# A hybrid decoder block on one core: in the MLP's first pass the product S1·T1 third and S2·T2 fourth, and a GpSimd power planned at 1.2 instead of 0.35

## The chip, the core and the metric

The kernel runs on one core of a Trainium2 chip. The metric is the device time of one execution in microseconds (us). Before the change it is 1147.73 us, the median of three runs (1147.73 to 1148.61). In this text TensorE is PE in the profile, VectorE is DVE, ScalarE is ACT, GpSimd is POOL, and SP is the engine whose queue issues the DMAs.

## What is computed

One decoder block over 1024 tokens of width 1024 with float32 data. `rms_norm` is x / sqrt(mean(x²) + eps) times a gain, and `sh`, `sc` and `gt` are shifts, scales and gates that a small product makes of the conditioning vector.

```python
h = rms_norm(x, g_attn_pre[l]) * (1 + sc_a) + sh_a
proj = h @ w_in[l]
...
mixed = jnp.concatenate([rms_norm(oa, g_mix_a[l]), rms_norm(ob, g_mix_b[l])], axis=-1)
y = mixed @ w_out[l]
x = x + gt_a * rms_norm(y, g_attn_post[l])

h = rms_norm(x, g_mlp_pre[l]) * (1 + sc_m) + sh_m
...
```

The last lines of the layer are the MLP: h times `w_up` (1024 x 4096), squared ReLU, times `w_down` (4096 x 1024), then a norm, a gate and a residual sum. oa and ob are the outputs of two kinds of attention.

## The kernel before

**Products.** Each float32 factor is split into a high part (a cast to the format fp32r, which TensorE multiplies) and a low part (the factor less its high part). A product is then three matmuls: high by high, high by low and low by high. High parts are casts on ScalarE (L1666 for a whole tile, L1664 for a piece of its columns); low parts are subtractions on VectorE (L1673, L1670). The function `split` makes both.

**Scheduling.** The program is written out by a list scheduler, the class `Sched`. Each piece of work is given to it by `op` (for ScalarE, VectorE, GpSimd), `pe_op` or `dense` (TensorE) or `load` (DMA), with the work that it depends on, the buffers that it takes and gives back, a priority and a duration that the author entered. The scheduler keeps a clock for each engine, and when an engine is free it appends the work that can start by these durations, by priority. Its choices fix the order of the instructions on each engine; on the chip every engine runs its own list in that order, and semaphores hold an instruction until what it needs is there. The planned durations have no other effect on what is executed.

**Output projection.** `out_block(tb)` is called for each of eight blocks of 128 tokens. For a block it loads the attention's output (`o_sb`), casts it on ScalarE (L1436), takes its low part on VectorE (L1439), squares it on ScalarE (L1441), sums on VectorE (L1445, L1446) and on TensorE (the matmuls `pm_o`, L1452), and after a small VectorE instruction (L1460) raises two columns to the power -1/2 on GpSimd (`rab`, L1462, planned at 0.5). TensorE makes y in tiles of 12 matmuls (L1478 to L1480); ScalarE (L1493) and VectorE (L1499) read them, scaled by `rab`. Then comes twice the helper `norm`: a sum of squares on ScalarE (L1506), a small VectorE instruction (L1515) and a power of one column on GpSimd (L1517, planned at 0.35). Between the two stand L1521 (scale and gate) and L1524 (add the residual x), after the second L1532 (`xn`, the scaled row). TensorE transposes xn (`px`, L1541, 8 matmuls), and VectorE or ScalarE writes the eight pieces of h, each with a scale and a shift (L1560, L1557). The blocks overlap, and the last ones overlap with the start of the MLP.

**MLP.** w_up and w_down are worked off in eight passes ("halves", h = 0 to 7), alternately a part of w_up and a part of w_down. In a pass both factors are 2 x 2 blocks, and instead of eight block products there are seven, P1 to P7, with sums of blocks as their factors (Winograd's variant of Strassen's scheme): `OPERANDS` names the pair of each, S for sums of the left factor's blocks, T for the right one's. S1 = A21 + A22, S2 = S1 - A11, S3 = A11 - A21, T1 = B12 - B11, T2 = B22 - T1. A product is 48 matmuls (L1902, L1903, L1904), in four PSUM banks (m = 0 to 3) by four blocks of the inner dimension. `ORDER` is the order of the products in a pass. In the first pass the left factor is h itself, so S1, S2 and S3 are made while the last h pieces are still coming. `first_sums` makes S1 (L1792) and S2 (L1797) in two pieces of columns, 384 and 128 wide per row of 512 (`PIECES`), for each of two halves j of the inner dimension, so that a part of each can be cast before the last token block is there; S3 is L1815. All other sums of blocks are whole tiles (`add_up`, L1835). The products' banks are read by `read_up` (ScalarE L1936, L1941, L1942 and VectorE L1939). The high and low parts of the left factor in the first pass are stored to DRAM by `store_parts` and loaded again in later passes. The tiles of w are loaded into a ring of buffers, and a slot is free when the sum or the split that reads it last is done.

In the first pass P2 runs bank by bank. `ml.seq` is the list of all products; `product` calls `sums` and `prep` for a product, `prep` calls `split`, and the priority of both follows from the product's place in `ml.seq`.

Of the kernel before, what the change touches and what calls it, by code (L numbers as in the profile page):

```python
# [20 lines left out]
D = 1024  # L21
# [327 lines left out]
def hybrid_block(ctx: ExitStack, tc: tile.TileContext, x, positions, w_ada, b_ada, g_attn_post, w_in, w_out,  # L349
# [1066 lines left out]
    def out_block(tb):  # L1416
# [92 lines left out]
        def norm(col, dep):  # L1509
            bx = []  # L1510

            def f1():
                t = small.tile([P, 8], F32, name="rs_t", tag="rs_t")
                bx.append(t)
                V.tensor_scalar(t[:, :1], b["st"][:, col:col + 1], 1.0 / D, EPS, ALU.mult, ALU.add)  # L1515
            e = op("DVE", 0.08, f1, [dep], prio=0)
            return op("POOL", 0.35, lambda: G.tensor_tensor(b["st"][:, col + 1:col + 2], bx[0][:, :1], nhalf[:, :1],  # L1517
                                                            ALU.pow), [e], prio=0)
        e = op("ACT", t_sb(D) + AP_COST, f_sq(0, True), ey, prio=1)
        e = norm(0, e)  # L1520
# [66 lines left out]

    NW = 4
    ORDER = ("P1", "P2", "P6", "P5", "P7", "P3", "P4")
    LAST = ("P1", "P2", "P6", "P5", "P3", "P7", "P4")  # L1590
    CHAIN = ("P1", "P6", "P7", "P4")
    OPERANDS = dict(P1=("11", "11"), P2=("12", "21"), P6=("S2", "T2"), P5=("S1", "T1"), P7=("S3", "T3"),
# [2 lines left out]
    BANKS = ([(pj, "pj", r_pj)] * 2 + [(psp, "s", r_s)] * 2,  # L1595
             [(po, "o", r_o), (px, "x", r_x), (pt, "t", r_t), (pt, "t", r_t)])
    ml = Tok()
    ml.seq = [(h, p) for h in range(2 * NW) for p in (ORDER if h < 2 * NW - 1 else LAST)]
    ml.fed = ml.begun = ml.done = 0
    ml.y, ml.e_y, ml.st = {}, {}, {}  # L1600
    halves = {}
    e_sd = {}
# [50 lines left out]
    def split(prio, rec, side, src, deps, free, pieces=None):  # L1653

        out = rec.hl[side] = [None, None]
        evs = [None, None]
        for i, c in enumerate(pieces or (slice(0, 512),)):
            for j in range(2):
                def hi(i=i, j=j, c=c):
                    if not i:  # L1660
                        i_, out[j] = new_pair()
                        rec.join[j].n.append(i_)
                    if pieces:
                        A.copy(halves_of(out[j][0])[:, :, c], pair(src[j])[:, :, c])  # L1664
                    else:
                        A.copy(out[j][0], flat(src[j]))  # L1666

                def lo(j=j, c=c):
                    if pieces:
                        V.tensor_tensor(halves_of(out[j][1])[:, :, c], pair(src[j])[:, :, c],  # L1670
                                        halves_of(out[j][0])[:, :, c].bitcast(F32), ALU.subtract)
                    else:
                        V.tensor_tensor(out[j][1], flat(src[j]), out[j][0].bitcast(F32), ALU.subtract)  # L1673

                def after(j=j):
                    for n in free:
                        n[j].hit()
                n = 2 * (c.stop - c.start)
                d = [deps(j)[i]] if pieces else deps(j)
                e1 = op("ACT", t_as(n), hi, d + (evs[j] or []), takes=[] if i else [(r_hl, 1)], prio=prio)  # L1680
                evs[j] = [e1, op("DVE", t_dv(n), lo, [e1], prio=prio,
                                 after=after if c.stop == 512 else None)]
        return evs
# [22 lines left out]
    def sums(h, p):  # L1706

        t = half(h)
        fr = t.free
        up_ = h % 2 == 0  # L1710
        own_a = h == 0 or not up_
        if p == "P1":
            fr.update({"T1": joins(r_raw, 2), "T3": joins(r_raw, 1), "B22": joins(r_raw, 3), "T4": joins(r_raw, 1),
                       "T2": joins(r_raw, 2)})
            if h == 0:
                t.a = {q: h2[q] for q in h2}
                t.e_a = dict(e_h2)
# [12 lines left out]
        ea, eb = events(h)  # L1730
        sum_ = partial(add_up, 10 + ml.seq.index((h, p)))
        if p == "P6":
            sum_(t.b, t.e_b, eb, r_raw, None, "T1", "12", "11", ALU.subtract, [], t.sp["B", "11"], "11")
            sum_(t.b, t.e_b, eb, r_raw, ring_r, "T2", "22", "T1", ALU.subtract, [fr["B22"], fr["T1"]], None, None)
            if h == 0:
                first_sums(t)
            elif own_a:
                sum_(t.a, t.e_a, ea, t.ring, t.new, "S1", "21", "22", ALU.add, [fr["A22"]], None, None)
                sum_(t.a, t.e_a, ea, t.ring, None, "S3", "11", "21", ALU.subtract, [], [[e] for e in t.e_a["S1"]], "21")
                sum_(t.a, t.e_a, ea, t.ring, None, "S2", "S1", "11", ALU.subtract, [fr["S1"]],  # L1740
                     [x + [t.e_a["S3"][j]] for j, x in enumerate(t.sp["A", "11"])], "11")
        if p == "P7":
            sum_(t.b, t.e_b, eb, r_raw, None, "T3", "22", "12", ALU.subtract, [fr["B22"]], [[e] for e in t.e_b["T1"]],
                 "12")
        if p == "P3" and own_a:
            sum_(t.a, t.e_a, ea, t.ring, None, "S4", "12", "S2", ALU.subtract, [fr["S2"]], t.sp["A", "12"], "12")
        if p == "P4":
            sum_(t.b, t.e_b, eb, r_raw, None, "T4", "21", "T2", ALU.subtract, [fr["T2"]], t.sp["B", "21"], "21")

    def prep(h, p, rec):  # L1750
# [11 lines left out]
        t.sp["B", b] = eB  # L1762
        if own_a:
            fa = [fr["A22"]] if a == "22" else [fr[a]] if a[0] == "S" else []
            eA = split(pr, rec, "A", t.a[a], (lambda j: t.e_a["S2"][j::2]) if (h, a) == (0, "S2") else ea(a), fa,
                       PIECES if (h, a) == (0, "S2") else None)
            t.sp["A", a] = eA
        else:
            eA = load_parts(rec, p)
# [9 lines left out]

    def first_sums(t):  # L1780

        pr = 10 + ml.seq.index((0, "P6"))
        for q in ("S1", "S2"):
            t.a[q] = [None, None]
        t.e_a.update(S1=[], S2=[], S3=[])
        last = {}
        for i, c in enumerate(PIECES):
            for j in range(2):
                def f_s1(i=i, j=j, c=c):
                    if not i:  # L1790
                        t.a["S1"][j] = ring_r("sum_S1")
                    V.tensor_tensor(pair(t.a["S1"][j])[:, :, c], t.a["21"][j][:, :, c], t.a["22"][j][:, :, c], ALU.add)  # L1792

                def f_s2(i=i, j=j, c=c):
                    if not i:
                        t.a["S2"][j] = ring_l("sum_S2", F32)
                    V.tensor_tensor(pair(t.a["S2"][j])[:, :, c], pair(t.a["S1"][j])[:, :, c], t.a["11"][j][:, :, c],  # L1797
                                    ALU.subtract)

                def after(i=i, j=j):  # L1800
                    if i:
                        t.free["S1"][j].hit()
                e1 = op("DVE", t_dv(2 * (c.stop - c.start)), f_s1, [t.e_a[q][2 + i] for q in ("21", "22")] +
                        [x for x in [last.get((1, j))] if x], takes=[] if i else [(r_h2, 1)], prio=pr,
                        after=t.free["A22"][j].hit if i else None)
                e2 = op("DVE", t_dv(2 * (c.stop - c.start)), f_s2, [e1, t.e_a["11"][3]] +
                        [x for x in [last.get((2, j))] if x], takes=[] if i else [(r_u, 1)], prio=pr, after=after)
                last[1, j], last[2, j] = e1, e2
                t.e_a["S2"].append(e2)
                if i:  # L1810
                    t.e_a["S1"].append(e1)
        t.a["S3"] = t.a["21"]
        for j in range(2):
            def f_s3(j=j):
                V.tensor_tensor(flat(t.a["21"][j]), flat(t.a["11"][j]), flat(t.a["21"][j]), ALU.subtract)  # L1815

            def after(j=j):
                sc_give(r_h2)
            t.e_a["S3"].append(op("DVE", t_dv(D), f_s3, [t.e_a["S1"][j]] + t.sp["A", "11"][j], prio=pr + 0.6,
                                  after=after))  # L1820

    def sc_give(r):
        r.give(sc.end)
# [44 lines left out]
    def product(h, p):  # L1868
# [7 lines left out]
        rec.join = [Join(None, [], 3 if h == 0 else 1) for _ in range(2)]  # L1876
        if not q:
            sums(h, p)
        prep(h, p, rec)
        ch = 0 if p in CHAIN else 1  # L1880
        banks = BANKS[ch if up_ else 1 - ch]
        starts, ends = p in ("P1", "P2", "P5"), p in ("P2", "P3", "P4")
# [197 lines left out]
```

## Time and profile before

| | |
|---|---|
| median of 3 runs | 1147.73 us |
| profiled execution, its own time | 1148.87 us |
| span of the profiled execution | 1147.1 us |
| mean granted TensorE clock | 0.992 |
| out of the seven products of the eight passes: matmuls on L1902, L1903 and L1904 | 896 each |
| power L1517: count, mean | 16, 838 ns |
| power L1462: count, mean | 8, 700 ns |

The times in the views are microseconds from the start of the span, unless they are marked ns. A row of a timeline has the start, the duration, the engine, the line, the operation, the tile written and those read, the shapes and a count of instructions that followed one another; a bracket has the idle time before and what ended it. A row of a group has the count, the busy time, the mean of one in ns and the idle time before with its releasers. Matmuls are pipelined, so consecutive matmuls overlap in the records and their distance is the difference of the starts. A row of the windows has the stretch, its length, the busy time of PE, PEld (the loading of weights), DVE, ACT and POOL with their counts, the granted clock of TensorE, the DMA share and GB/s.

### The profile page before, as it was taken

What the parts mean: (1) busy time and instruction counts of PE and PEld (TensorE: products, weight loads), DVE (VectorE), ACT (ScalarE), POOL (GpSimd) and SP (SyncE); (2) the same over time, 40 slices, a digit from 0 to 9 for tenths busy, and PEclk for the clock granted to TensorE, in tenths of its full rate; (3) what the DMA queues carried; (4) which work ended last, traced back from release to release, by engine and by line L of the source; (5) the groups of instructions that cost most, each with busy time, mean ns of one, the idle gap of its engine ahead of it and who ended that gap; (6) DMA issues with size and microseconds to landing.
All of it is one profiled execution on the core that took longest, in us unless ns stands there. A gap on an engine that the chain in (4) does not pass through costs nothing.

```text
span 1147.1 us, 15609 instructions
## 1 busy us (share of the span) xinstructions
PE 1115.2 (97%) x5417; PEld 924.1 (81%) x5417; DVE 818.7 (71%) x1380; ACT 635.9 (55%) x1101; POOL 265.7 (23%) x349
## 2 busy tenths in 40 slices
PE   8999999999999899998999999999999999999996
PEld 7788878888888687887788888888888888888885
DVE  7878666666667765668979664599644896537998
ACT  8868865464556756675675424563234733246542
POOL 2458867565743521111000000000000000000002
PEclk9999999999999899998999999999999999999999
DMA  9556454343423305552981168812469112584103
GB/s 347 192 204 164 163 158 164 136 155 127 146 71 132 124 26 186 203 207 104 352 306 39 41 224 285 303 37 74 147 230 332 70 56 76 201 307 168 37 19 147
DMA packets 90910, 185.29 MB, mean 162 GB/s; under 512 B 8400, under 2 KB 31056, under 8 KB 90832
## 3 DMA queue, kind: packets, MB, share of 16 engines
q1 hardware_dynamic: 90832, 184.30, 46.3%
q8 instruction: 43, 0.70, 0.2%
q14 instruction: 35, 0.29, 0.1%
HBM read 137.08 MB, written 28.31 MB: 144 GB/s over the span
## 4 chain that ended last, share of the span: by engine, by line
PE 76%; DVE 8%; issue 4%; ACT 4%; POOL 4%; DMA 3%; SPq 1%; DVEq 0%; POOLq 0%; ACTq 0%
PE mlp_ps L1903 16%; PE mlp_ps L1904 16%; PE mlp_ps L1902 16%; PE pj L866 3%; PE pj L869 3%; PE pj L867 3%; PE s_ps L1127 3%; PE o_ps L1262 2%; PE pt_ps L1232 1%; PE y_ps L1478 1%; PE y_ps L1480 1%; PE y_ps L1479 1%; PE pt_ps L1235 1%; DVE hw L1673 1%; PE o_ps L1267 1%
## 5 line engine op out<-in xcount | busy, mean ns | idle before, releaser
L1902 PE MATMUL mlp_ps<-hw 128*128 128x512 f32 x896 | 350.7, 391 | 0.4 <-ACT hw L1664 0.4
L1903 PE MATMUL mlp_ps<-hw 128*128 128x512 f32 x896 | 349.5, 390 | 1.1 <-DVE hw L1670 1.1
L1904 PE MATMUL mlp_ps<-hw 128*128 128x512 f32 x896 | 349.4, 390 | 0.0
L1903 PEld LDWEIGHTS mlp_ps<-hw 128*128 128x128 f32 x896 | 168.7, 188 | 36.9 <-DVE hw L1670 1.4
L1902 PEld LDWEIGHTS mlp_ps<-hw 128*128 128x128 f32 x896 | 168.8, 188 | 36.4 <-ACT hw L1664 0.8
L1904 PEld LDWEIGHTS mlp_ps<-hw 128*128 128x128 f32 x896 | 168.6, 188 | 35.0
L1673 DVE TENSOR_TENSOR hw<-w,hw 128x1024 fp32r<-128x1024 f32 x96 | 114.7, 1221 | 95.1 <-ACT hw L1666 93.0
L1666 ACT CAST hw<-w 128x1024 fp32r<-128x1024 f32 x96 | 97.5, 1047 | 129.8 <-PE mlp_ps L1904 93.1
L2002 POOL TENSOR_TENSOR st<-st,nhalf 128x1 f32<-128x1 f32 x8 | 7.8, 977 | 604.1 <-DVE st L2000 604.1
L866 PE MATMUL pj<-hw,w_hl 128*128 128x512 f32 x240 | 102.5, 427 | 0.0
L869 PE MATMUL pj<-hw,w_hl 128*128 128x512 f32 x240 | 94.6, 394 | 0.0
L867 PE MATMUL pj<-hw,w_hl 128*128 128x512 f32 x240 | 94.5, 394 | 0.0
L1250 DVE TENSOR_TENSOR ph<-pt_ps,ph 128x512 fp32r<-128x512 f32 (+1 forms) x110 | 69.5, 648 | 34.6 <-ACT ph L1246 34.3
L1666 ACT CAST hw<-u 128x1024 fp32r<-128x1024 f32 x48 | 48.7, 1051 | 64.6 <-PE mlp_ps L1904 64.6
L1246 ACT CAST ph<-pt_ps 128x512 fp32r<-128x512 f32 (+1 forms) x110 | 58.9, 555 | 32.9 <-PE pt_ps L1235 27.5
L1153 ACT ACTIVATE p_sb<-p_sb,mn 128x128 f32<-128x128 f32 (+3 forms) x64 | 49.8, 778 | 38.3 <-DVE mn L1146 36.8
L1673 DVE TENSOR_TENSOR hw<-u,hw 128x1024 fp32r<-128x1024 f32 x48 | 57.1, 1220 | 18.2 <-ACT hw L1666 18.2
L1960 DVE TENSOR_TENSOR yacc<-yacc,mlp_ps 128x512 f32<-128x512 f32 x96 | 62.2, 683 | 3.3 <-PE mlp_ps L1904 3.3
L1158 POOL TENSOR_SCALAR p_sb<-p_sb,den 128x128 f32<-128x128 f32 (+3 forms) x64 | 48.4, 762 | 53.1 <-DVE den L1156 51.9
L1015 POOL TENSOR_TENSOR ada_acc<-ada_acc,wa_st 128x512 f32<-128x512 f32 x42 | 55.3, 1318 | 3.5
L869 PEld LDWEIGHTS pj<-hw,w_hl 128*128 128x128 f32 x240 | 45.1, 188 | 10.5
L1478 PE MATMUL y_ps<-hw,oh 128*128 128x512 f32 x128 | 51.7, 404 | 0.0
(206 smaller groups left out, 2010.4 us busy)
## 6 DMA issues: line engine op xcount, KB each, us to landing
hw<-s_dram SPq DMA_DIRECT2D x84, 512.0 KB, 4.4
wa_st<-in_w_ada SPq DMA_DIRECT2D x32, 512.0 KB, 4.4
w<-in_w_up SPq DMA_DIRECT2D x32, 512.0 KB, 4.8
w<-in_w_down SPq DMA_DIRECT2D x32, 512.0 KB, 7.5
s_dram<-hw SPq DMA_DIRECT2D x28, 512.0 KB, 4.3
qt<-hl SPq DMA_DIRECT2D x40, 256.0 KB, 2.8
w_st<-in_w_in SPq DMA_DIRECT2D x36, 256.0 KB, 3.1
x_sb<-in_x SPq DMA_DIRECT2D x16, 512.0 KB, 6.1
```

What stands on the lines that cost most here:

```text
L866: T.matmul(ps, w[:, 0, n], h[0], start=(k == 0), stop=False)
L867: T.matmul(ps, w[:, 1, n], h[0], start=False, stop=False)
L869: T.matmul(ps, w[:, 0, n], h[1], start=False, stop=(k == KC - 1))
L1246: A.copy(b["ph"][:, 0, :w], b["pt"][:, :w])
L1250: V.tensor_tensor(b["ph"][:, 1, :w], b["pt"][:, :w], b["ph"][:, 0, :w].bitcast(F32), ALU.subtract)
L1478: T.matmul(ps[:], b["oh"][:, k], wh[:, c0:c0 + 512], start=(k == 4 * m), stop=False)
L1666: A.copy(out[j][0], flat(src[j]))
L1673: V.tensor_tensor(out[j][1], flat(src[j]), out[j][0].bitcast(F32), ALU.subtract)
L1902: T.matmul(ps[m][:], sh, mh, start=starts and k == 0, stop=False, **kw)
L1903: T.matmul(ps[m][:], sh, ml_, start=False, stop=False, **kw)
L1904: T.matmul(ps[m][:], sl, mh, start=False, stop=k == 3, **kw)
L1960: e = op("DVE", t_dv(512), lambda: V.tensor_tensor(y(), y(), ps[m][:], ALU.add), [e, ml.e_y[tb, n]], gives=gives, prio=1)
```

## The change

The first pass has an order of its own, `FIRST_UP`, in which P5 (S1·T1) is third and P6 (S2·T2) fourth; the other passes keep theirs. T1's sum goes with P5 in the first pass. `first_sums` is cut in two: S1, in its two pieces of columns, is made ahead of P5; `second_sums` makes S2, now as two whole tiles, and S3 behind it. `prep` splits S1 in pieces in place of S2. In `split`, for priorities below 17 (products in the first pass), the first casts of a product depend, for the scheduler, on the first casts of the product before it having been placed (`ml.turn`, `rec.turn`); this makes no semaphore. Both powers of `norm` (L1517) are planned at 1.2 instead of 0.35.

```diff
-            return op("POOL", 0.35, lambda: G.tensor_tensor(b["st"][:, col + 1:col + 2], bx[0][:, :1], nhalf[:, :1],
+            return op("POOL", 1.2, lambda: G.tensor_tensor(b["st"][:, col + 1:col + 2], bx[0][:, :1], nhalf[:, :1],
...
     ORDER = ("P1", "P2", "P6", "P5", "P7", "P3", "P4")
+    FIRST_UP = ("P1", "P2", "P5", "P6", "P7", "P3", "P4")
...
-    ml.seq = [(h, p) for h in range(2 * NW) for p in (ORDER if h < 2 * NW - 1 else LAST)]
+    ml.seq = [(h, p) for h in range(2 * NW) for p in (FIRST_UP if not h else ORDER if h < 2 * NW - 1 else LAST)]
+    ml.turn = []
...
+        turn = ml.turn if prio < 17 else []
...
-                e1 = op("ACT", t_as(n), hi, d + (evs[j] or []), takes=[] if i else [(r_hl, 1)], prio=prio)
+                mine = Ev()
+                if not i:
+                    rec.turn.append(mine)
+                e1 = op("ACT", t_as(n), hi, d + (evs[j] or turn), takes=[] if i else [(r_hl, 1)], prio=prio,
+                        after=partial(setattr, mine, "t", 0.0))
...
+        if p == ("P6" if h else "P5"):
+            sum_(t.b, t.e_b, eb, r_raw, None, "T1", "12", "11", ALU.subtract, [], t.sp["B", "11"], "11")
+            if not h:
+                first_sums(t)
         if p == "P6":
-            sum_(t.b, t.e_b, eb, r_raw, None, "T1", "12", "11", ALU.subtract, [], t.sp["B", "11"], "11")
             sum_(t.b, t.e_b, eb, r_raw, ring_r, "T2", "22", "T1", ALU.subtract, [fr["B22"], fr["T1"]], None, None)
             if h == 0:
-                first_sums(t)
+                second_sums(t)
...
-            eA = split(pr, rec, "A", t.a[a], (lambda j: t.e_a["S2"][j::2]) if (h, a) == (0, "S2") else ea(a), fa,
-                       PIECES if (h, a) == (0, "S2") else None)
+            eA = split(pr, rec, "A", t.a[a], (lambda j: t.e_s1[j::2]) if (h, a) == (0, "S1") else ea(a), fa,
+                       PIECES if (h, a) == (0, "S1") else None)
...
-                def f_s2(i=i, j=j, c=c):
-                    if not i:
-                        t.a["S2"][j] = ring_l("sum_S2", F32)
-                    V.tensor_tensor(pair(t.a["S2"][j])[:, :, c], pair(t.a["S1"][j])[:, :, c], t.a["11"][j][:, :, c],
-                                    ALU.subtract)
...
+    def second_sums(t):
+
+        pr = 10 + ml.seq.index((0, "P6"))
+        t.a["S2"] = [None, None]
+        t.e_a.update(S2=[], S3=[])
         t.a["S3"] = t.a["21"]
+        for j in range(2):
+            def f_s2(j=j):
+                t.a["S2"][j] = ring_l("sum_S2", F32)
+                V.tensor_tensor(t.a["S2"][j][:], flat(t.a["S1"][j]), flat(t.a["11"][j]), ALU.subtract)
+            t.e_a["S2"].append(op("DVE", t_dv(D), f_s2, [t.e_a["S1"][j], t.e_a["11"][3]], takes=[(r_u, 1)], prio=pr,
+                                  after=t.free["S1"][j].hit))
...
+        rec.turn = []
         prep(h, p, rec)
+        ml.turn = rec.turn
```

More of the change, by code (lines that the diff above doesn't have):

```diff
@@ L1780, in first_sums @@
     def first_sums(t):
[L1782 to L1785, printed above, removed]
+        pr = 10 + ml.seq.index((0, "P5"))
+        t.a["S1"] = [None, None]
+        t.e_s1 = []
         last = {}
@@ L1792, in f_s1 @@
                     V.tensor_tensor(pair(t.a["S1"][j])[:, :, c], t.a["21"][j][:, :, c], t.a["22"][j][:, :, c], ALU.add)
-                def f_s2(i=i, j=j, c=c):
-                    if not i:
-                        t.a["S2"][j] = ring_l("sum_S2", F32)
-                    V.tensor_tensor(pair(t.a["S2"][j])[:, :, c], pair(t.a["S1"][j])[:, :, c], t.a["11"][j][:, :, c],
-                                    ALU.subtract)
-                def after(i=i, j=j):
-                    if i:
-                        t.free["S1"][j].hit()
                 e1 = op("DVE", t_dv(2 * (c.stop - c.start)), f_s1, [t.e_a[q][2 + i] for q in ("21", "22")] +
-                        [x for x in [last.get((1, j))] if x], takes=[] if i else [(r_h2, 1)], prio=pr,
+                        [x for x in [last.get(j)] if x], takes=[] if i else [(r_h2, 1)], prio=pr,
                         after=t.free["A22"][j].hit if i else None)
[L1806 to L1811, printed above, removed]
-        t.a["S3"] = t.a["21"]
+                last[j] = e1
+                t.e_s1.append(e1)
+        t.e_a["S1"] = t.e_s1[2:]
+    def second_sums(t):
+        pr = 10 + ml.seq.index((0, "P6"))
+        t.a["S2"] = [None, None]
+        t.e_a.update(S2=[], S3=[])
+        t.a["S3"] = t.a["21"]
+        for j in range(2):
[4 more added lines that the diff above has]
+                                  after=t.free["S1"][j].hit))
         for j in range(2):
@@ L1818, in after @@
                 sc_give(r_h2)
-            t.e_a["S3"].append(op("DVE", t_dv(D), f_s3, [t.e_a["S1"][j]] + t.sp["A", "11"][j], prio=pr + 0.6,
-                                  after=after))
+            t.e_a["S3"].append(op("DVE", t_dv(D), f_s3, [t.e_a["S1"][j], t.e_a["S2"][j]] + t.sp["A", "11"][j],
+                                  prio=pr + 0.6, after=after))
     def sc_give(r):
```

## The prediction

> **What bounds the kernel now.** The page first: TensorE is busy for 97% of the span, and the chain of work that ended last lies on it for three quarters.
>
> ```profile
> PE 1115.2 (97%) x5417; PEld 924.1 (81%) x5417; DVE 818.7 (71%) x1380; ACT 635.9 (55%) x1101; POOL 265.7 (23%) x349
> PE 76%; DVE 8%; issue 4%; ACT 4%; POOL 4%; DMA 3%; SPq 1%; DVEq 0%; POOLq 0%; ACTq 0%
> ```
>
> So only TensorE's idle time can be gained, or time at a lower clock. The sum of its waits over 395 to 600 us (the output projection and the MLP's first pass) lists all that is idle where the change works:
>
> ```profile
> PE px L1541 <- ACT xn L1532: 5.1, 3, 3.1
> PE mlp_ps L1903 <- DVE hw L1670: 1.1, 1, 1.1
> PE mlp_ps L1902 <- ACT hw L1664: 0.4, 1, 0.4
> PE pm_o L1452 <- DVE o_sb L1446: 0.2, 1, 0.2
> ```
>
> TensorE's timeline places them (start, duration, line; in brackets the idle time before and its releaser):
>
> ```profile
> 439.83 1.10 PE L1541 MATMUL px<-head,xn 128*128 128x128 f32 x8 [1.60 <-ACT xn L1532]
> ...
> 517.25 1.09 PE L1541 MATMUL px<-head,xn 128*128 128x128 f32 x8 [0.44 <-ACT xn L1532]
> ...
> 525.69 0.39 PE L1902 MATMUL mlp_ps<-hw 128*128 128x512 f32 x1
> ...
> 528.19 0.39 PE L1904 MATMUL mlp_ps<-hw 128*128 128x512 f32 x1
> 531.63 1.97 PE L1541 MATMUL px<-head,xn 128*128 128x128 f32 x8 [3.06 <-ACT xn L1532]
> ...
> 533.83 0.63 PE L1903 MATMUL mlp_ps<-hw 128*128 128x512 f32 x1
> ...
> 537.67 0.42 PE L1903 MATMUL mlp_ps<-hw 128*128 128x512 f32 x1
> ...
> 545.42 0.39 PE L1904 MATMUL mlp_ps<-hw 128*128 128x512 f32 x1
> 546.17 0.50 PE L1902 MATMUL mlp_ps<-hw 128*128 128x512 f32 x1 [0.36 <-ACT hw L1664]
> 547.79 0.50 PE L1903 MATMUL mlp_ps<-hw 128*128 128x512 f32 x1 [1.12 <-DVE hw L1670]
> 548.13 0.40 PE L1904 MATMUL mlp_ps<-hw 128*128 128x512 f32 x1
> ```
>
> The px at 517.25 and 531.63 are the transposes of token blocks 6 and 7, inside P1 and P2. Eleven matmuls lie from 525.69 to 528.19: 0.227 apart, the full pace. The two bracketed waits at the third product, 546.17 and 547.79, are S2's casts and low parts. The windows show that the long stall costs more than its own length:
>
> ```profile
> 440.00:450.00 10.00, 9.89 (x49) 8.08 (x49) 7.53 (x14) 6.68 (x12) 1.50 (x3) 1.00 0.41 151
> ...
> 531.00:532.00 1.00, 0.37 (x2) 0.37 (x3) 0.00 (x0) 1.00 (x3) 0.00 (x0) 0.50 0.00 0
> ...
> 537.00:538.00 1.00, 1.00 (x5) 0.77 (x4) 0.45 (x1) 0.16 (x1) 0.00 (x0) 0.64 0.00 0
> 538.00:539.00 1.00, 1.00 (x6) 0.83 (x5) 1.00 (x2) 0.70 (x2) 0.00 (x0) 1.00 0.00 0
> ```
>
> The third number from the right is the granted clock: 0.50 from the stall to about 537.7, but 1.00 after the idle 1.60 at 439.83. At the lower clock px took 1.97 and not 1.09 (0.8 of it on the path), and ten matmuls ran 0.427 apart (nine steps from 533.83 to 537.67), 0.2 more each, 2.0 together: the clock cost about 2.8.
>
> The cause of the 3.06 is on GpSimd and VectorE:
>
> ```profile
> 514.56 1.45 POOL L1517 TENSOR_TENSOR st<-rs_t,nhalf 128x1 f32<-128x1 f32 x1 [7.14 <-DVE rs_t L1515]
> 526.94 3.46 POOL L1517 TENSOR_TENSOR st<-rs_t,nhalf 128x1 f32<-128x1 f32 x1 [6.00 <-DVE rs_t L1515]
> ```
>
> ```profile
> 515.53 1.40 DVE L1499 SCALAR_TENSOR_TENSOR y_sb<-y_ps,rab,y_sb 128x512 f32<-128x512 f32 x2
> ...
> 526.72 0.15 DVE L1515 TENSOR_SCALAR rs_t<-st 128x1 f32<-128x1 f32 x1
> 526.78 2.35 DVE L1835 TENSOR_TENSOR sum_T<-w,w 128x1024 f32<-128x1024 f32 x2
> 529.05 0.95 DVE L1792 TENSOR_TENSOR sum_S<-h,h 128x768 f32<-128x768 f32 x1
> ```
>
> A power of one column (L1517) takes 3.46: it ends at 530.40, 0.40 after the third of three VectorE operations that ran behind its L1515 (529.05 + 0.95 = 530.00). At 514.56 it was held by one and took 1.45. xn and px follow only then.
>
> **The change part by part.**
>
> *The power's cost.* With 1.2 instead of 0.35 nothing runs longer; the list scheduler places what follows the power later. I read the instruction order of the changed program for this. Block 7's px now stand behind 12 of P2's matmuls, not 3, so TensorE gets there 9 x 0.227 = 2.0 later. Block 6's px also stand later, and its 0.44 goes. On VectorE the second L1515 of block 7 has between it and the L1499 pair the same full-size operations as before plus one S1 sum of 0.95; before, that stretch was 526.72 - 516.93 = 9.8, so now about 10.7.
>
> At an earlier place the order gets worse. There pm_o L1452 of block 3 moves 9 matmuls ahead (36 now stand between it and the px at 439.83, 45 before), while the sums in front of it come no sooner:
>
> ```profile
> 446.53 1.23 DVE L1524 TENSOR_TENSOR y_sb<-y_sb,x_sb 128x1024 f32<-128x1024 f32 x1
> ...
> 451.41 0.43 DVE L1446 TENSOR_TENSOR o_sb<-o_sb 128x256 f32<-128x256 f32 x1
> ```
>
> ```profile
> 449.58 1.06 ACT L1441 ACTIVATE o_sb<-o_sb 128x1024 f32<-128x1024 f32 x1 [0.58 <-DVE ol L1439]
> 450.55 0.67 ACT L1493 ACTIVATE y_sb<-y_ps,rab 128x512 f32<-128x512 f32 x1
> ```
>
> ```profile
> 451.98 0.58 PE L1452 MATMUL pm_o<-ones,o_sb 128*128 128x1 f32 x4
> ```
>
> In the new order L1439 and L1524 (1.2 each) stand right behind block 2's L1460, which starts the power L1462. L1439 is running when the power falls due, and L1524 waits for nothing but a load long landed and VectorE itself; if both hold the power up, it ends near 449.0. ScalarE's L1493 (0.67) waits for it, and the square L1441 (1.06) that L1445 and L1446 need is queued behind L1493, the other way round than in the rows; with the two sums (1.1) L1446 ends near 452.0, while TensorE is there at 449.9 (px at 439.83 plus 0.85, 36 matmuls and one pm_o). That is a new stall of 2.1, on the path. If the power gets in between the two it is 0.4 to 1.1. I take 2.1, since the row at 526.94 is the nearest. px and pm_o, now apart, cost 0.2 more than together, an estimate from the starts around them.
>
> *The product order.* Each product still issues 48 matmuls, 10.9 at 0.227, so their sum stays. S1 needs one sum where S2 needed a sum and a subtraction behind it:
>
> ```profile
> L1835 DVE TENSOR_TENSOR sum_T<-w,w 128x1024 f32<-128x1024 f32 x16 | 19.2, 1220 | 0.1
> L1797 DVE TENSOR_TENSOR sum_S<-sum_S,h 128x768 f32<-128x768 f32 x2 | 1.9, 950 | 0.0
> L1797 DVE TENSOR_TENSOR sum_S<-sum_S,h 128x256 f32<-128x256 f32 x2 | 0.8, 420 | 0.0
> ```
>
> The four pieces of L1797 (2.7 in all) become two whole subtractions of 1.22 (2.4), needed one product later: 10.9 of S1·T1 covers them. Without stalls the third product's third matmul would start three steps of 0.227 after the one at 545.42, at 546.1; it started at 548.13. So 2.0 goes if S1's pieces are ready, and P5 keeps some 0.4 on its fourth bank, whose reader is late. They should be: behind block 7's px come eight h pieces, S1's last columns, a cast and a low part, about 5, and 36 matmuls of P2 (8.2) stand there. Casts held by the new turn lists only change places on ScalarE, which has idle time in that stretch; the w_down loads that SP's queue now issues ahead of S1's stores are used in the next half, up to 76 later (7 x 10.9), and its stores are read there too. S2·T2's last operand, the second T2, now waits for a ring slot; by the new order and the rows' durations its low part comes 0.7 ahead of its matmul. I cost it at nothing; a microsecond more there is a microsecond on the path.
>
> *Where the power goes now.* P1 starts 2.1 later, and VectorE's stretch is 0.9 longer, so the last L1515 comes at 526.72 + 2.1 + 0.9 = 529.7 or a little before. Behind it stand S1's second piece (0.95), two low parts of T1 (1.22 each) and a T2 sum (1.22). TensorE reaches px near 532.4 (528.42, where it was free before, plus 2.1 + 0.2 - 0.4 and the nine matmuls). So all depends on how many of the four the power must sit out. At the kernel's end two got in:
>
> ```profile
> 1116.79 2.13 POOL L2002 TENSOR_TENSOR st<-st,nhalf 128x1 f32<-128x1 f32 x2 [586.39 <-DVE st L2000]
> ```
>
> ```profile
> 1116.69 0.68 DVE L1997 TENSOR_TENSOR yg<-yacc,gate_m 128x512 f32<-128x512 f32 x1
> 1117.30 2.35 DVE L1673 TENSOR_TENSOR hw<-u,hw 128x1024 fp32r<-128x1024 f32 x2
> ```
>
> The two powers from 1116.79 end at 1118.92, while the two L1673 behind L1997 run on to 1119.65: each got in ahead of a low part that waits on another engine's semaphore. The row at 526.94 shows three operations that waited for no other engine (the loads of their operands had landed), and none let it in. The first low part of T1 waits on TensorE, so the nearest row is L1673: the power ends 0.4 after S1's piece, near 531.0. ScalarE has two reads of P1's banks ahead of xn, over at about 531.6; xn takes 1.15:
>
> ```profile
> 531.49 1.05 ACT L1936 COPY u<-mlp_ps 128x512 f32<-128x512 f32 x2
> ```
>
> ```profile
> L1532 ACT ACTIVATE xn<-y_sb,st 128x1024 f32<-128x1024 f32 x8 | 9.2, 1149 | 5.7 <-POOL st L1517 5.7
> ```
>
> px starts at 532.8, an idle time of 0.3 and no loss of clock. One low part more costs 1.1, within the idle lengths that kept the clock. If all four hold it, it ends at 534.4, px comes at 535.6, and the stall is 3.1 again, clock and all.
>
> The Trainium skill bears on this: its page "SBUF — State Buffer", section "Who interferes with whom", says that a VectorE instruction with two SBUF inputs and a GpSimd instruction that reads SBUF exclude one another, and that issue order decides who waits. The long L1517 agree with the exclusion. By issue order alone the waiting power would get in after one operation, as I take it; at 526.94 it sat out three, so the measurement decides that this is not sure.
>
> *The sum*, against the profiled execution's own 1148.87: block 6's px -0.4, block 7's px 3.06 to 0.3 -2.8, clock -2.8, third product -2.0, P5's bank +0.4, pm_o's stall +2.1, px and pm_o apart +0.2: -5.3, so 1143.6. That execution lies 1.1 above the median of 1147.73; on the median's terms 1142.4. After the first pass the order on each engine is as before and TensorE is the bound, so the gain lasts to the end.
>
> **The rivals** (microseconds on the median's terms).
>
> *A second stall as long as the first.* All four operations hold the power: the px and clock terms vanish, and -0.4 - 2.0 + 2.1 + 0.2 leaves about 0: 1147.5. For it: 526.94. Against it: the semaphore waits.
>
> *No stall at pm_o.* The power L1462 gets through, so 1.0 to 2.1 less: near 1140.6. For it: L1439, too, is a low part; against it: it has already begun.
>
> *S2·T2 waits in its place.* The change doesn't do what it says: the 2.0 comes back at the fourth product, through the late second T2: 1144.4. Against it: a slack of 0.7 and, for S2 itself, 10.9.
>
> *Slower: the clock falls at pm_o.* An idle 2.1 lies between 1.60, which kept the clock, and 3.06, which lost it, so it can cost the 2.8 of the first stall there. Together with the second stall at px, the same mechanism (powers held by VectorE's two-input operations) gives 0 + 2.8: 1150.3. It decides from an idle time of somewhat over 2 at pm_o. For it: both places have an unbroken run of such operations. With only the first it would be 1145.2, still faster.
>
> The Trainium skill's "TensorE: Matmul & The Clock Gate", section "Part 1: The HAM clock gate (the "warmup" mystery)", puts the idle window at about 3.4 us. Here 3.06 of idle time lost the clock, so the measurement decides against that figure; by it no stall here would cost clock, and the second stall would give 1144.7.
>
> **How the numbers follow.** Forecast 0.46; no stall at pm_o 0.10; S2·T2 waits 0.07; second stall 0.20; slower 0.17, with what I have not seen. About 0.2% (2.3) is what a measurement here can tell from no change. The first three are faster, 0.63; the second stall is the same, 0.20; the last slower, 0.17. The forecast's own range is 1141 to 1145 (a low part more, a shorter stall at pm_o, the clock at pm_o). For 8 in 10 I reach to 1139.8 below and 1149.6 above, which takes in the second stall whole and leaves out most of the slower case.
>
> **What would show it.** Right: block 7's px in P2 after a wait under 1, the granted clock 1.00 from 528 to 540, no wait on L1664 or L1670 at the third product, a wait of about 2 at pm_o near 450, and the last L1517 about 1.3 long. Wrong: an L1517 over 4 there, a granted clock of 0.50 near 450 or 534, or waits in the fourth product.

## The result, and the profile after

| | before | after |
|---|---|---|
| median in one batch, us (runs) | 1148.41 (7) | 1144.1 (7) |
| profiled execution, own time / span | 1148.87 / 1147.1 | 1144.1 / 1142.2 |
| block 0's px to the second pass's first matmul (the 337th on L1902 to L1904) | 162.31 | 158.15 |

The ratio is 0.9969, with a 95% interval of 0.996 to 0.9978: 3.6 us faster (the two medians lie 4.3 apart). The third row is a cleaner measure than the span, since block 0's px starts anywhere from 438.3 to 442.8 over the profiles of these kernels. Its two ends before are 439.83 and 602.14, and after 439.13 and 597.28. From there to the end both take the same time: the spans differ by 4.9, as the second mark does, and 0.7 of that lies ahead of block 0's px, within that scatter.

TensorE's timeline after, with the rows that answer to those of before (the matmuls' lines are now L1912 to L1914):

```profile
439.13 1.09 PE L1541 MATMUL px<-head,xn 128*128 128x128 f32 x8 [1.51 <-ACT xn L1532]
449.64 0.58 PE L1452 MATMUL pm_o<-ones,o_sb 128*128 128x1 f32 x4 [0.42 <-DVE rs_t L1515]
516.79 1.03 PE L1541 MATMUL px<-head,xn 128*128 128x128 f32 x8
...
529.01 0.39 PE L1914 MATMUL mlp_ps<-hw 128*128 128x512 f32 x1
532.31 1.97 PE L1541 MATMUL px<-head,xn 128*128 128x128 f32 x8 [2.91 <-ACT xn L1532]
533.93 0.78 PE L1912 MATMUL mlp_ps<-hw 128*128 128x512 f32 x1
534.50 0.63 PE L1913 MATMUL mlp_ps<-hw 128*128 128x512 f32 x1
534.93 0.60 PE L1914 MATMUL mlp_ps<-hw 128*128 128x512 f32 x1
535.36 0.41 PE L1912 MATMUL mlp_ps<-hw 128*128 128x512 f32 x1
...
542.65 0.39 PE L1914 MATMUL mlp_ps<-hw 128*128 128x512 f32 x1
542.88 0.39 PE L1912 MATMUL mlp_ps<-hw 128*128 128x512 f32 x1
543.11 0.39 PE L1913 MATMUL mlp_ps<-hw 128*128 128x512 f32 x1
```

Block 6's px (516.79) no longer wait. Block 7's (532.31) still wait 2.91, nearly the 3.06 of before, and still take 1.97; but only three matmuls behind them are slow, not ten. P2 ends with the row at 542.65, and the third product follows at the full step of 0.23. The windows of after (third number from the right: granted clock):

```profile
531.00:532.00 1.00, 0.00 (x0) 0.00 (x0) 0.00 (x0) 0.89 (x1) 0.08 (x1) 0.98 0.00 0
532.00:535.00 3.00, 2.69 (x11) 2.50 (x12) 1.53 (x5) 2.88 (x6) 0.00 (x0) 0.50 0.00 0
535.00:536.00 1.00, 1.00 (x5) 0.81 (x4) 1.00 (x2) 1.00 (x4) 0.00 (x0) 0.81 0.00 0
```

In a slice of 1 us a mean of 0.98 between 1.00 and 0.50 means 0.04 us at the low clock. So the clock fell at 531.96 and came back at 535.38: 3.42 us. Before, it was low for 6.82: from 530.90, by the slice of before below, to 537.72, by the 0.64 from 537 to 538.

```profile
530.00:531.00 1.00, 0.00 (x0) 0.00 (x0) 0.00 (x0) 0.57 (x1) 0.40 (x1) 0.95 0.00 0
```

GpSimd and VectorE after:

```profile
445.02 1.62 POOL L1462 TENSOR_TENSOR rab<-rs_t,nhalf 128x2 f32<-128x2 f32 x1 [1.47 <-DVE rs_t L1460]
...
526.49 4.59 POOL L1517 TENSOR_TENSOR st<-rs_t,nhalf 128x1 f32<-128x1 f32 x1 [7.40 <-DVE rs_t L1515]
```

```profile
444.86 1.22 DVE L1439 TENSOR_TENSOR ol<-o_sb,oh 128x1024 fp32r<-128x1024 f32 x1
445.99 1.22 DVE L1524 TENSOR_TENSOR y_sb<-y_sb,x_sb 128x1024 f32<-128x1024 f32 x1
...
526.26 0.15 DVE L1515 TENSOR_SCALAR rs_t<-st 128x1 f32<-128x1 f32 x1
526.32 0.95 DVE L1801 TENSOR_TENSOR sum_S<-h,h 128x768 f32<-128x768 f32 x1
527.19 2.36 DVE L1676 TENSOR_TENSOR hw<-w,hw 128x1024 fp32r<-128x1024 f32 x2
529.46 1.22 DVE L1843 TENSOR_TENSOR sum_T<-w,w 128x1024 f32<-128x1024 f32 x1
```

The last power takes 4.59: it was kept out by all four operations behind its L1515 (S1's piece, two low parts of T1, a T2 sum) and ended at 531.08, 0.40 after the fourth (530.68). At 445.02 the other power got in behind the first of two such operations: it ended at 446.64, and L1524 ran until 447.21. The same power gets in at the same place in pow, plan and two64 (1.62 each).

Where the 4.16 between the marks came from, as differences of starts in the two timelines: block 6's px 0.7, block 7's px 0.15, the clock 1.4 (0.8 on px is still paid, seven slow matmuls of 0.2 are not), the third product 2.0; given back 0.16 in the output projection. That is 4.1. The 1.4 of the clock can't be put down to the change: by the last section it depends on where the stall fell on a raster of 3.41 us in these two executions. Without it they differ by 2.8.

### The profile page after: what moved, and what is told of

Same layout as the page of the kernel before. It is cut to its first block, busy times and chain, and to the rows that moved or that the text cites. A ratio compares the mean times of both kernels' runs of the same rounds, so it can differ in the third digit from the quotient of the medians.

```text
span 1142.2 us, 15600 instructions
## 1 busy us (share of the span) xinstructions
PE 1113.5 (97%) x5417; PEld 925.2 (81%) x5417; DVE 819.3 (72%) x1378; ACT 636.1 (56%) x1101; POOL 267.8 (23%) x349
## 4 chain that ended last, share of the span: by engine, by line
PE 77%; DVE 8%; ACT 4%; issue 4%; POOL 3%; DMA 3%; SPq 0%; DVEq 0%; POOLq 0%; ACTq 0%
PE mlp_ps L1913 17%; PE mlp_ps L1914 17%; PE mlp_ps L1912 17%; PE pj L866 4%; PE pj L869 4%; PE pj L867 4%; PE s_ps L1127 3%; PE o_ps L1262 2%; PE y_ps L1478 1%; PE pt_ps L1232 1%; PE y_ps L1479 1%; PE y_ps L1480 1%; PE pt_ps L1235 1%; DMA o_sb<-o_dram 1%; PE o_ps L1267 1%
## 5 line engine op out<-in xcount | busy, mean ns | idle before, releaser
L1912 PE MATMUL mlp_ps<-hw 128*128 128x512 f32 x896 | 349.8, 390 | 0.0
L1914 PE MATMUL mlp_ps<-hw 128*128 128x512 f32 x896 | 348.8, 389 | 0.0
L1912 PEld LDWEIGHTS mlp_ps<-hw 128*128 128x128 f32 x896 | 168.5, 188 | 35.5 <-issue 0.5
L1914 PEld LDWEIGHTS mlp_ps<-hw 128*128 128x128 f32 x896 | 168.4, 188 | 34.9
```

The source lines that it names most:

```text
L1912: T.matmul(ps[m][:], sh, mh, start=starts and k == 0, stop=False, **kw)
L1914: T.matmul(ps[m][:], sl, mh, start=False, stop=k == 3, **kw)
```

## The experiments

Theory: the last power is kept out as long as VectorE runs operations with two SBUF inputs one right behind the other, and that alone makes block 7's stall; the product order gains the 2.0 of S2's waits by itself. Rivals are named with the runs. "Marks" is the time from block 0's px to the second pass, "power" the last one's duration, "wait" block 7's px, "clock low at px" the low stretch there. All four come from one profiled execution of each kernel. In gate_b and best the marks also hold a loss of clock at block 0's px. A kernel with one run has no ratio and stands for its trace alone. Kernels with an added small instruction have the power at L1518.

| kernel | median, us (runs) | before in its batch (runs) | ratio, 95% | marks | power | wait | clock low at px |
|---|---|---|---|---|---|---|---|
| order | 1146.3 (12) | 1148.88 (23) | 0.9977, 0.9965 to 0.9989 | 159.15 | 4.33 | 3.25 | 3.42 |
| pow | 1148.56 (12) | 1148.88 (23) | 0.9993, 0.9983 to 1.0004 | 160.01 | 4.06 | 2.63 | 3.41 |
| gate | 1141.44 (6) | 1148.88 (23) | 0.9935, 0.992 to 0.9949 | 154.38 | 1.18 | 0.19 | none |
| gate_o | 1142.81 (6) | 1148.88 (23) | 0.9949, 0.9932 to 0.9965 | 155.75 | 1.19 | 1.47 | none |
| gap | 1142.08 (4) | 1147.61 (13) | 0.9946, 0.993 to 0.9961 | 153.90 | 1.19 | 0.22 | none |
| gap0 | 1139.5 (1) | 1147.61 (13) | | 153.86 | 1.19 | 0.19 | none |
| two | 1139.24 (1) | 1147.61 (13) | | 153.96 | 1.20 | 0.20 | none |
| gate_b | 1147.04 (10) | 1147.61 (13) | 0.9994, 0.9983 to 1.0004 | 161.34 | 1.45 | 1.70 | none |
| best | 1141.6 (5) | 1148.49 (9) | 0.994, 0.9926 to 0.9953 | 154.82 | 1.18 | 0.18 | none |
| plan | 1147.62 (1) | 1148.49 (9) | | 159.72 | 4.59 | 3.59 | 6.82 |
| two64 | 1147.22 (1) | 1148.49 (9) | | 158.71 | 4.73 | 3.72 | 3.4 |
| two256 | 1143.25 (1) | 1148.49 (9) | | 156.21 | 3.79 | 2.79 | none |

**The two halves of the change: "order" and "pow".** "order" is the kernel after with the power planned at 0.35 again; "pow" is the kernel before with 1.2.

```diff
-            return op("POOL", 1.2, lambda: G.tensor_tensor(b["st"][:, col + 1:col + 2], bx[0][:, :1], nhalf[:, :1],
+            return op("POOL", 0.35, lambda: G.tensor_tensor(b["st"][:, col + 1:col + 2], bx[0][:, :1], nhalf[:, :1],
```

> The product order alone, the power planned at 0.35 as before. If the power sits out the whole unbroken run of VectorE's two-input operations: the last L1517 is 4.2 to 4.7 long (two S1 pieces of 0.9 and two low parts of T1 of 1.14 stand behind its L1515), block 7's px wait 3.2 to 3.6 and lose the clock again, only the third product's waits (2.0) go, and the time is 1.5 to 2.2 under the kernel before. If it gets in ahead of a low part that waits on another engine, as the prediction had it: L1517 is 2.2 long, px wait about 1, the clock stays 1.00, and the time is 5.5 to 7 under before. In both there is no new wait at pm_o.

> The power planned at 1.2 alone, products in the order of before. Sat-out theory: the last L1517 is 4.1 to 4.5 long (a T2 sum, two S1 pieces and an S2 piece behind its L1515), px wait 2.6 to 3.2 behind 12 of P2's matmuls, the wait at pm_o is 0.4 as in the changed kernel, and the third product S2·T2 still waits about 2. Time 0.5 to 2 under before. Get-in theory: L1517 is 3.3 long, px wait under 2 without loss of clock, time 3 to 4.5 under before.

GpSimd's timeline of order, and then TensorE's waits from 395 to 600 in pow (sum, count, longest):

```profile
529.90 4.33 POOL L1517 TENSOR_TENSOR st<-rs_t,nhalf 128x1 f32<-128x1 f32 x1 [6.00 <-DVE rs_t L1515]
```

```profile
PE px L1541 <- ACT xn L1532: 4.3, 2, 2.6
PE mlp_ps L1903 <- DVE hw L1670: 1.1, 1, 1.1
PE mlp_ps L1902 <- ACT hw L1664: 0.7, 1, 0.7
```

The power is long in both (4.33 and 4.06), again until 0.40 after a run of four two-input operations. S2's two waits stay in pow and are gone in order. The order of the products alone is worth 2.6 (0.23%); the entered duration alone, 0.07%, can't be told from nothing. By the marks order is 3.2 and pow 2.3 below before, but there, too, part is the clock, low for 3.4 and not 6.82.

**Letting the power in: "gate" and "gate_o".** One VectorE instruction of one column is put behind the first operation that holds the power. It copies the power's result, so it waits for it. For the scheduler this power is planned at 0.1, so that the instruction lands there. gate is made of after, gate_o of order.

```diff
+            late_ = tb == TB - 1 and col == 2
-            return op("POOL", 1.2, lambda: G.tensor_tensor(b["st"][:, col + 1:col + 2], bx[0][:, :1], nhalf[:, :1],
-                                                            ALU.pow), [e], prio=0)
+            ep = op("POOL", 0.1 if late_ else 1.2, lambda: G.tensor_tensor(b["st"][:, col + 1:col + 2], bx[0][:, :1],
+                                                                             nhalf[:, :1], ALU.pow), [e], prio=0)
+            if late_:
+                op("DVE", 0.08, lambda: V.tensor_copy(bx[0][:, 2:3], b["st"][:, col + 1:col + 2]), [ep], prio=-20)
+            return ep
```

> The changed kernel and one small VectorE copy of the last power's result, which stands behind the first of the four operations that held the power, so that VectorE waits there for GpSimd; that power is planned at 0.1. Theory that px wait because VectorE's two-input operations keep GpSimd's power from its operands: L1517 falls from 4.6 to 1.2, VectorE idles about 0.4, px wait under 0.6, the clock stays 1.00 from 528 to 545, and the time is 3.5 to 4.5 under the changed kernel. Rival, that xn is late because of ScalarE's own queue (casts and bank reads ahead of it): px still wait over 2 and the time is within 0.5 of the changed kernel. Rival, that VectorE is the bound behind px: px come early but the third product waits for S1's low parts, and less than half of the 4 is gained.

> The product order alone (power planned at 0.35) with the same small copy behind the first operation. The power theory: L1517 about 1.2, px (now ahead of P2's first matmul, since that power is planned at 0.1) wait 1 to 1.6, the clock stays, and the time is 5 to 6.5 under before, 0.5 to 2 over the kernel with the copy and 1.2: what 1.2 itself is worth once the power is not held. ScalarE rival: px wait about 3 as in the kernel before, time 2 under before.

TensorE's waits of gate from 526 to 600:

```profile
PE mlp_ps L1916 <- DVE u L1953: 0.6, 1, 0.6
PE px L1545 <- ACT xn L1536: 0.2, 1, 0.2
```

With the power at 1.18 the stall falls from 2.91 to 0.19 and no clock is lost; between the marks it is 3.77 less than after, 3.5 of it from these (2.7 of stall, 1.4 of clock, less 0.6 of a new wait for a bank's reader at L1916). So the held power makes nearly the whole stall (2.7 of 2.9), and the rival that ScalarE's own queue delays xn falls.

**What lets it in: "gap", "gap0", "two".** Two rivals: VectorE must wait for the power by a semaphore (gap and gap0 take that wait away); or an operation with a single SBUF input must come between (two has two inputs). gap copies L1515's output; gap0 copies a constant, which is there long before, so that it also takes away that the instruction becomes ready late; two adds two columns.

```diff
-                op("DVE", 0.08, lambda: V.tensor_copy(bx[0][:, 2:3], b["st"][:, col + 1:col + 2]), [ep], prio=-20)
+                op("DVE", 0.08, lambda: V.tensor_copy(bx[0][:, 2:3], bx[0][:, :1]), [ep], prio=-20)
...
+                op("DVE", 0.08, lambda: V.tensor_copy(bx[0][:, 2:3], nhalf[:, :1]), [ep], prio=-20)
...
+                op("DVE", 0.08, lambda: V.tensor_tensor(bx[0][:, 2:3], bx[0][:, :1], nhalf[:, :1], ALU.add), [ep], prio=-20)
```

> The kernel with the copy, but the small VectorE copy reads L1515's output (one SBUF input) and so doesn't wait for the power; order of all engines as with the waiting copy. If only an unbroken run of two-input operations holds the power, one instruction with a single input breaks it: L1517 1.2, px wait under 0.6, clock 1.00, and the time as with the waiting copy or 0.2 to 0.4 under it. If the power is held until VectorE has nothing more to issue: L1517 4.6 to 4.8, px wait over 3 (TensorE now arrives three matmuls earlier), clock lost, time within 1 of the changed kernel.

> As the run before, but the small copy reads a constant and waits for nothing, so that it can be issued long before. If a single input is what matters: the same as the run before (L1517 1.2). If it matters that an instruction becomes ready only after the one ahead of it has begun (L1515's output does): L1517 4.6 to 4.8 here and 1.2 in the run before.

> As the run before the last, but the small instruction adds L1515's output and a constant: two SBUF inputs, and it becomes ready only after S1's piece ahead of it has begun. If a single input is what matters: the power is held to the end of the run, L1517 4.6 to 4.8. If readiness is what matters: L1517 1.2.

VectorE's and then GpSimd's timeline of two:

```profile
525.35 0.94 DVE L1805 TENSOR_TENSOR sum_S<-h,h 128x768 f32<-128x768 f32 x1
526.22 0.15 DVE L1521 TENSOR_TENSOR rs_t<-rs_t,nhalf 128x1 f32<-128x1 f32 x1
526.29 2.35 DVE L1680 TENSOR_TENSOR hw<-w,hw 128x1024 fp32r<-128x1024 f32 x2
```

```profile
525.51 1.20 POOL L1518 TENSOR_TENSOR st<-rs_t,nhalf 128x1 f32<-128x1 f32 x1 [7.40 <-DVE rs_t L1515]
```

VectorE has no idle time in these rows, the small add reads two SBUF columns, and still the power ends at 526.71, while the first low part runs. gap0's small copy and its power:

```profile
526.49 0.14 DVE L1521 COPY rs_t<-nhalf 128x1 f32<-128x1 f32 x1
```

```profile
525.78 1.19 POOL L1518 TENSOR_TENSOR st<-rs_t,nhalf 128x1 f32<-128x1 f32 x1 [7.40 <-DVE rs_t L1515]
```

The copy ends at 526.63, the power at 526.97. Both rivals fall: it needs neither a wait nor a single input, nor an instruction that becomes ready late.

**The same on the kernel before: "gate_b".** The diff is that of gate, with 0.35 for the other powers.

> The kernel before (products and planned power as before) with the waiting copy behind the first T2 sum. Power theory: L1517 1.5 instead of 3.5, px wait 1.5 to 2 and not 3.06, no loss of clock. The third product S2·T2 then comes earlier than its S2, whose chain starts from the same px: its waits grow from 1.5 to 2.5 to 4, and the time is 1.5 to 3.5 under before. So the product order would be worth 2 to 4 once the power is not held. If S2's waits stay at 1.5, it is worth 2.

TensorE's timeline of gate_b at the third product:

```profile
540.98 0.39 PE L1908 MATMUL mlp_ps<-hw 128*128 128x512 f32 x1
542.33 0.50 PE L1906 MATMUL mlp_ps<-hw 128*128 128x512 f32 x1 [0.97 <-ACT hw L1668]
543.71 0.50 PE L1907 MATMUL mlp_ps<-hw 128*128 128x512 f32 x1 [0.88 <-DVE hw L1674]
544.04 0.40 PE L1908 MATMUL mlp_ps<-hw 128*128 128x512 f32 x1
...
544.89 0.63 PE L1908 MATMUL mlp_ps<-hw 128*128 128x512 f32 x1
545.32 0.63 PE L1906 MATMUL mlp_ps<-hw 128*128 128x512 f32 x1
```

The power is short (1.45) and block 7's px keep the clock, but the expected gain of 1.5 to 3.5 is not seen: 0.06% can't be told from nothing. In the profile S2's waits are 1.85, less than expected, but lose the clock there (steps of 0.43 from 544.89), and block 0's px lost it too, behind an idle 2.06. Compared with gate_o, the two product orders differ by 5.6 between the marks once the power is let in; about 1.3 of it is the clock at block 0's px, which neither edit touches (76.7 against 75.4 from there to P1's first matmul). By the ratios, each against before in its own batch, they differ by 0.45 points, about 5.

**Best, and its control: "best" and "plan".** best is gap0 again, timed. plan has the planned 0.1 without the small instruction.

> The kernel gap0 again, for its time: the changed kernel and one small VectorE copy of a constant behind the first of the operations that held the power, which is planned at 0.1. L1517 1.2, px wait 0.2, clock 1.00; the time 7 to 8.5 under the kernel before, 3 to 5 under the changed kernel. If the copy only shifts the stall to the fourth or a later product, half of that.

> Control: the last power planned at 0.1 and no small instruction; otherwise the order of gap0. If the small instruction is what lets the power in: L1517 4.6, px wait 3.4 to 3.7 (TensorE arrives three matmuls earlier than in the changed kernel), clock lost. If it was the planned cost that did it: L1517 1.2 and px wait 0.2.

GpSimd's timeline of plan:

```profile
528.07 4.59 POOL L1518 TENSOR_TENSOR st<-rs_t,nhalf 128x1 f32<-128x1 f32 x1 [7.40 <-DVE rs_t L1515]
```

With 0.1 alone the power takes 4.59, as in after: it is the instruction that lets it in, not the plan. best is 0.6% below before, about 7 us; gate, gap and best lie 0.23 to 0.34 points below after by their ratios, each against before in its own batch, and the interval of best (0.9926 to 0.9953) lies wholly below that of after (0.996 to 0.9978).

**How small must it be: "two64" and "two256".** The added instruction has 64 or 256 columns; it writes a tile that nothing reads any more.

```diff
+                op("DVE", 0.133, lambda: V.tensor_tensor(ph2.gate[:, :64], ph2.gate[:, :64], ph2.gate[:, 64:128], ALU.add), [ep], prio=-20)
```

> In place of the small instruction one with two SBUF inputs of 64 elements per partition. The power got in around one element of two inputs. If what lets it in is a gap between two streams of operands, which a short instruction leaves because its fixed time is longer than its stream: 64 elements stream for about 0.07 at the rate of the 1024-element operations (1.14 for 1024), as long as the distance of two small instructions, so the gap is near closed: either answer, L1517 1.2 to 1.3 or 4.6. If any extra instruction lets it in: 1.2 to 1.3.

> As two64 with 256 elements (about 0.33); two low parts of T1 follow it, and T2's sum has moved behind the px. Gap theory: held through all of them, L1517 0.87 + 0.33 + 1.14 + 1.22 + 0.4 - 0.16 = 3.8. If any extra instruction lets it in: 1.2 (before it) or 1.5 (behind it).

VectorE's timeline of two64, then GpSimd's:

```profile
528.55 0.94 DVE L1805 TENSOR_TENSOR sum_S<-h,h 128x768 f32<-128x768 f32 x1
529.41 0.21 DVE L1521 TENSOR_TENSOR gate_a<-gate_a 128x64 f32<-128x64 f32 x1
529.55 2.35 DVE L1680 TENSOR_TENSOR hw<-w,hw 128x1024 fp32r<-128x1024 f32 x2
531.82 1.22 DVE L1847 TENSOR_TENSOR sum_T<-w,w 128x1024 f32<-128x1024 f32 x1
```

```profile
528.71 4.73 POOL L1518 TENSOR_TENSOR st<-rs_t,nhalf 128x1 f32<-128x1 f32 x1 [7.40 <-DVE rs_t L1515]
```

At 64 columns (0.21) the power is kept out to the end of the run, 0.40 after 533.04. At 256 it is too; its 3.79 is shorter because the scheduler moved the T2 sum behind px. So one column opens the way and 64 do not. Size is not all that differs: two64 and two256 work on another tile (gate_a) than the one-column instructions, which write the tile that the power reads (rs_t). A small instruction on another tile was not run, and each of these two kernels ran once. That one column takes 0.15 while reading its operands should need far less (64 columns take 0.21 and 1024 take 1.22, so about 0.001 a column, an estimate), so that the reading of operands pauses, fits this, but is argued and not shown.

## Why the prediction held, and where it did not

The direction and the range held, but by its own signs the mechanism at block 7's px was wrong: of the signs of being right only the third product without waits came; the wait of 2.91, the power of 4.59, the clock of 0.50 near 534 and the short wait at pm_o all went the other way. On the profile -5.3 was forecast and about -4.1 came between the marks, since errors offset each other: 4.0 too much gain at block 7's px and its clock, 2.1 too much loss in the output projection (1.7 of it at pm_o), 0.4 for a bank and 0.3 too little at block 6's px. The first two are linked, and that they met is luck: without the stall at pm_o TensorE stood at block 7's px at 529.4 and not near 532.4, and the last L1515 started at 526.26 and not near 529.7; the power then was held over 3 longer than forecast. So px started 93.18 after block 0's px, where 92.97 was forecast, with a stall of 2.91 in place of the two.

- **The product order** held: no wait at the third product, 2.0 gained; order and pow show that it comes from the order of the products alone. The fourth product has no wait for T2 either, so that rival falls.
- **Block 6's px** held: its 0.44 went.
- **"Where the power goes now"** failed. The step let the power in ahead of the first low part of T1, since that waits on another engine, and took -2.8 for px and -2.8 for the clock. All four operations held it, as in the rival of a second stall: px gave -0.15, and the clock -1.4 in this execution. A semaphore on the next instruction is not what opens the way: both low parts carry one and neither opened it, while the small adds and copies of two and gap0 opened it and were over before the power, so that they didn't wait for it. What opened it here is a one-column instruction between two long ones.
- **pm_o's stall** was mis-sized: +2.1 against a measured 0.42. The power L1462 got in between L1439 and L1524, and its 0.4 was the lower bound that the step named. So a power was let in between two full-size operations there, and not between two like them behind 526.49; why, no run here settles.
- **The clock at px** was priced as all or nothing (2.8 or 0); it cost 1.4 in the execution after.
- **P5's bank** (+0.4) did not show in after. It came as 0.6 at L1916 in gate, once the stall was gone.

So the rival "a second stall as long as the first" was right in its mechanism and wrong in its sum: its 0 becomes about -4, since the output projection gave back 0.16 and not 2.3, the clock was lost for half as long (1.4), and px of blocks 6 and 7 gained 0.4 more.

The Trainium skill's page "SBUF — State Buffer", section "Who interferes with whom", says that a VectorE instruction with two SBUF inputs and a GpSimd one that reads SBUF lock one another out and that issue order decides who blocks. The lock-out agrees with every long row here. Issue order does not: the power of after began at 526.49, and the three operations from 527.19 on went ahead of it for 3.5 us.

## What to carry to other kernels

A short GpSimd operation on the critical path should not fall due inside a run of long VectorE operations with two SBUF inputs: look for its longest row beside its mean (3.46 beside 0.838 before), and try a one-column VectorE instruction behind the first operation that holds it. A duration entered in a planner moved other work and did not shorten the wait (4.06 in pow). When one price in a sum is taken from the nearest row and that row is one of two kinds, keep the other kind's outcome as a case with every other term recomputed, since here it gained too.

## What the runs showed of the hardware

**Around these px, the clock falls by the idle time inside one of the fixed windows of 3.41 us.** The low stretches around the changes last 3.41 to 3.42 or 6.82, and their starts lie on one raster. In after they start within these slices and at 531.96:

```profile
149.00:150.00 1.00, 1.00 (x7) 0.86 (x7) 0.94 (x4) 0.97 (x3) 1.00 (x4) 0.83 0.20 80
392.00:393.00 1.00, 0.73 (x3) 0.73 (x4) 1.00 (x5) 0.29 (x1) 0.92 (x2) 0.51 0.71 147
```

By the clock in them the starts are 149.66 and 392.02; the distances 242.36 and 139.94 are 71.0 and 41.0 times 3.413. The length of a stall alone doesn't decide. best lost the clock behind 2.09 of idle time at block 0's px; TensorE's timeline and a window of best:

```profile
440.79 1.97 PE L1545 MATMUL px<-head,xn 128*128 128x128 f32 x8 [2.09 <-ACT xn L1536]
```

```profile
440.00:441.00 1.00, 0.21 (x1) 0.21 (x2) 1.00 (x2) 0.76 (x2) 0.00 (x0) 0.91 0.91 269
```

two256 kept it behind 2.79 at block 7's px. The windows of two256, then TensorE's timeline:

```profile
394.00:395.00 1.00, 0.80 (x6) 0.63 (x5) 1.00 (x6) 0.76 (x1) 1.00 (x1) 0.73 0.83 266
...
530.00:535.00 5.00, 2.75 (x16) 2.44 (x17) 2.67 (x7) 3.95 (x8) 1.01 (x1) 1.00 0.00 0
```

```profile
532.25 1.09 PE L1545 MATMUL px<-head,xn 128*128 128x128 f32 x8 [2.79 <-ACT xn L1536]
```

The start at 394.46 plus 40 windows is 530.99, which cuts the idle stretch from 529.46 to 532.25 into 1.53 and 1.26. In best the 2.09 lies wholly in the window that ends at 440.82, where the clock falls. On this count 1.70 in one window (block 7's px in gate_b) kept the clock and 1.85 (gate_b's two waits together) lost it, so the limit lies near 1.8 here, if two waits simply add up. It is not sharp, and not the same everywhere: order kept the clock with 1.85 (block 0's px waited until 442.82, in a window from 440.97), and before lost it at 394.37, in the attention's last products, where TensorE was busy for 1.75 of the window's 3.41, an idle time of 1.66. How long it stays low fits the raster too: before's stall ran on for 0.73 in the window from 530.90, and the clock was low for two windows; after's ran on for 0.35 in the one from 531.96, and it was low for one. The drop comes at the window's end, which can be after the stall. In order, too, the px wait 3.25, and start at 535.47; its windows are:

```profile
536.00:537.00 1.00, 1.00 (x8) 0.90 (x6) 0.84 (x3) 1.00 (x3) 0.00 (x0) 0.77 0.00 0
```

The clock falls at 536.54, 1.1 behind the stall. The Trainium skill's "TensorE: Matmul & The Clock Gate", section "Part 1: The HAM clock gate (the "warmup" mystery)", gives the free-running window as 3413 ns, which agrees; it also has the clock fall after at least one idle window of about 3.4 us, and here the 2.09 of best were enough. For a price it means: stalls of 2.8 to 3.1 us cost nothing (two256), 1.4 (after) or 2.8 (before), by where they fall on the raster.
